# Hybrid decoder block on one core: two weight-gain sums moved within the first projection, the rotary tables moved behind the first value head

## The chip, the core and the metric

The kernel runs on one core of a Trainium2 chip. The metric is the device time of one execution in microseconds; before the change it is 2252.84 us, the median of three runs (2250.17 to 2253.78). The engines of the core work through queues of their own: PE (TensorE: matrix products and transposes), DVE (VectorE: elementwise work), ACT (ScalarE: copies, casts and functions), POOL (GpSimd: elementwise work, and a queue that issues loads) and SP (SyncE: a queue that issues loads). Each takes its instructions in the order in which they were written into its queue.

## The reference, cut to what matters

One decoder block on 512 tokens of width 2048. The condition `c` gives six vectors of 2048 (shift, scale and gate, for each half of the block); the normalised input, scaled and shifted by them, goes through one projection into attention heads (`aq`, `ak`, `av`) and heads of a gated recurrence (`gq`, `gf`, `gi`, `gg`). Queries and keys of the attention get a rotary embedding on their first 32 channels.

```python
mod = silu(c) @ w_ada + b_ada
shift1, scale1, gate1, shift2, scale2, gate2 = split(mod, 6)
h = rms_norm(x, norm1_w) * (1 + scale1) + shift1
aq, ak, av, gq, gf, gi, gg = split(h @ w_in, ...)
ang = pos[..., None] * inv_freq            # 16 frequencies
aq = rope_partial(rms_norm(aq), cos(ang), sin(ang)); ak likewise
attn = dilated_attention(aq, ak, av)
ho = hgrn2(gq, gf, gi, lb)                 # gated recurrence
x = x + gate1 * (concat(attn, norm(ho) * silu(gg)) @ w_out)
x = x + gate2 * (square(relu((rms_norm(x, norm2_w) * (1 + scale2) + shift2) @ w_ff1)) @ w_ff2)
```

## The kernel before

Every float32 product is done as three products of rounded parts: a weight tile is split into `whi` (a cast on ACT) and `wlo` (the rest, on DVE), the input tile into `hi` and `lo`, and PE adds hi·whi, lo·whi and hi·wlo. The input dimension of 2048 is worked through in 16 tiles `k` of 128.

**The first projection** (`first_steps`, lines 730 to 908) makes the first four forget-gate heads (four banks `bt`, 512 columns) and two query heads (two banks `bc`, 256 columns). Its order on PE, SP, ACT and DVE is that of the code, as it stands under a manual schedule; POOL's is set by the planner. The weights are scaled by `g1c`, one value per input channel, which is norm1 times (1 + scale1). Because `g1c` comes itself out of a product with `w_ada`, it is made in eight blocks `b` of 256 channels while the projection runs: block `b` gives `g1c` for the tiles k = 2b and 2b + 1, and `split_w(k)` (line 757) can start only when it is there. Blocks 0, 1, 3, 5 and 7 are summed on PE: `summed` (line 792) multiplies, and `summed_out` (line 801) copies the sums out on ACT (line 803), transposes them on PE (line 806), reduces them on DVE (line 807) and calls `finish_scale` (two small DVE instructions, lines 813 and 814). Blocks 2, 4 and 6 are summed on DVE: `gathered` (line 816) does 16 scaled additions, and `gathered_out` (line 826) has four PE transposes and four ACT sums (`to_cols`, lines 144 and 147), then `finish_scale`. `fetch_block` (line 740) issues a block's eight loads on SP, `fetch_pair` (line 752) the projection's weights on POOL.

`dense(k)` (line 865) is the projection's product for one tile, in three runs of six matmuls: hi·whi, lo·whi, hi·wlo. What is handed in as `between` is issued before the third run. `split_x` splits the input tiles (cast on ACT, rest on DVE), `turn_x` transposes an input tile on PE and copies it out. The loop over pairs at line 880 puts these together; b = k0 / 2 + 1 is the block that the next pair needs.

`shift_steps(n)` (line 876) takes n steps of a background list: the sums for `shift1` on DVE, one step being one load of 128x512 on SP (line 117) and one scaled addition (lines 122 and 124), with transposes and ACT sums after each 16 (lines 144, 147). There are four such blocks of 512 channels. The **second projection** (`first_groups`, line 247) follows with the same input tiles and takes eight steps per pair; as a block of shifts is done, `shifted` (line 278) rewrites the input tiles with the shift in. Its PE work ends with the transposes of the last block. The **first value projection** (line 1006, `project(5120)`, "value head") uses the shifted tiles; its evacuation is at line 346. Behind the first projections, the planner orders DVE, ACT and POOL by the code's order as priority, with its own estimate of times, and gives out the buffers; PE's order from line 1004 on is that of the code.

**The rotary tables** (lines 962 to 995) stand between the two first projections: the angles, reduced in range, on DVE (28 instructions on 128x64 and smaller, most of them on the tile `rp`), two sines on ACT (lines 985, 986), `sinT` and `cosT` on DVE, and eight products with the norm weights on POOL into `rot_w` (line 995). Three of the eight buffers of the pool `wk` (512 columns each) hold `cosT`, `sinT` and `rp`. `rot_w` is first read by `qk_norm` (line 362), for the first query heads behind line 1011. The recurrent heads (`hgrn_head`, line 520) take their tiles `kk`, `Sx`, `z` and `mt` from the same pool.

Of the kernel before, what the change touches and what calls it, by code (L numbers as in the profile page):

```python
# [8 lines left out]
F32 = mybir.dt.float32  # L9
F32R = mybir.dt.float32r  # L10
I32 = mybir.dt.int32
AF = mybir.ActivationFunctionType
ALU = mybir.AluOpType
AX = mybir.AxisListType

P = 128
D = 2048
S = 512
NK = D // P
NT = S // P  # L20
# [5 lines left out]
MAGIC = 12582912.0  # L26
PI2 = 6.283185307179586
PI2_1 = 6.28125
PI2_2 = 0.0019350051879882812
PI2_3 = 3.019916050073166e-07  # L30
# [18 lines left out]
def hybrid_block(ctx, tc, x, c, positions, norm1_w, w_ada, b_ada, w_in, q_norm_w, k_norm_w,  # L49
# [3 lines left out]
    pe, dve, act, pool = nc.tensor, nc.vector, nc.scalar, nc.gpsimd  # L53
# [14 lines left out]
    ca = pa.enter_context(tc.tile_pool(name="ca", bufs=1))  # L68
# [31 lines left out]
    n2c, aoc, hgc, posc = cols[:, 0:16], cols[:, 16:24], cols[:, 40:41], cols[:, 44:48]  # L100
    rw = ca.tile([P, 2, 32], F32, name="rw")
# [3 lines left out]
    ifq = ca.tile([P, 16], F32, name="ifq")  # L105
# [125 lines left out]
    def work(name, dt=F32):  # L231
        return wk.tile([P, 512], dt, name=name, tag="wk")
# [403 lines left out]
    def hgrn(fs, qs, vs, rs, lead=0):  # L636
        ss = sm.tile([P, 4, NT], F32, name="hss", bufs=2)
        for h in range(4):
            yield from hgrn_head(h, fs[h], qs[h], vs, ss, 0 if h else lead)
        rstd_of(rs.rearrange("p t h -> p (t h)"), ss.rearrange("p t h -> p (t h)"), 16, 1.0 / DH)  # L640
# [89 lines left out]
    def first_steps(c_f, c_q):  # L730
# [7 lines left out]
        on_pe = (0, 1, 3, 5, 7)  # L738
# [18 lines left out]
        def split_w(k):  # L757
            parts[k] = [_split(nc, wr, raw[:, k % 2], raw.shape[2], None, g1c[:, k:k + 1]) for raw in wraws[k - k % 2]]

        def split_x(ks):  # L760
            for k in ks:
                hl = pair(k)
                hhi.append(hl[0])
                hlo.append(hl[1])
                split_to(hl, xnT[k])
# [18 lines left out]
        def turn_x(q, j, tag="bg"):  # L784
            pt = bank("ptx", tag=tag)
            for ti in range(NT):
                pe.transpose(pt[:, ti * P:(ti + 1) * P], xs[ti][q][:, j * P:(j + 1) * P], ident)
            t = slot("xnT")
            (dve.tensor_copy if q == 1 else act.copy)(t, pt)
            xnT.append(t)  # L790
# [25 lines left out]
        def gathered(b, ks):  # L816
            if b not in accs:
                accs[b] = [work("acc")[:, 0:256] for _ in range(2)]
            for k in ks:
                raw, acc = raws[b][k // 2][:, k % 2], accs[b][k % 2]  # L820
                if k < 2:
                    dve.tensor_scalar(acc, raw, sc[:, k:k + 1], None, op0=ALU.mult)
                else:
                    dve.scalar_tensor_tensor(acc, raw, sc[:, k:k + 1], acc, op0=ALU.mult, op1=ALU.add)
# [40 lines left out]
        def dense(k, between=None):  # L865
            fine, coarse = parts.pop(k)
            first, last = k == 0, k == NK - 1
            for n, (hs, w) in enumerate(((hhi, 0), (hlo, 0), (hhi, 1))):
                for banks, ws in ((bt, fine), (bc, coarse)):
                    for j in range(len(banks)):  # L870
                        pe.matmul(banks[j], lhsT=ws[w][:, j * P:(j + 1) * P], rhs=hs[k], start=first and n == 0,  # L871
                                  stop=last and n == 2)
                if n == 1 and between:
                    between()

        def shift_steps(n):
            for _ in range(n):
                bg_step()

        for k0 in range(0, NK, 2):  # L880
            b = k0 // 2 + 1
            if k0 + 4 < NK:
                fetch_pair(k0 + 4)
            if b < 8 and b not in on_pe:
                gathered(b, range(8, NK))
            if 0 < k0 < NK - 2:
                split_x((k0 + 2, k0 + 3))
            if k0 in (0, 4):
                scale_x(2 + k0 // 4, range(NT))
            dense(k0, lambda: turn_x(2 + k0 // 6, (k0 - 2) % 4) if 2 <= k0 <= 8 else None)  # L890
            if k0 in (0, 4, 10):
                summed((1, 3, 7)[k0 // 4], range(4))
            if 2 <= k0 <= 8:
                turn_x(2 + k0 // 6, (k0 - 2) % 4 + 1)
            shift_steps(5 if k0 == 10 else 0)
            dense(k0 + 1, lambda: None if b > 7 else (summed_out if b in on_pe else gathered_out)(b))
            if k0 == 6:
                summed(5, range(4))
            if b + 2 < 8:
                fetch_block(b + 2)  # L900
            if k0 + 2 < NK:
                split_w(k0 + 2)
                if b + 1 < 8 and b + 1 not in on_pe:
                    gathered(b + 1, range(8))
                shift_steps(4 if k0 >= 10 else 0)
                split_w(k0 + 3)
        shift_steps(4)
# [29 lines left out]
    with tc.issue_after(mod_cols.last.ins):  # L937
        posf = ca.tile([NT, P], F32, name="posf")
        dve.tensor_copy(posf, posi)
        ps_v = bank("ps_v")  # L940
        pe.transpose(ps_v[:, 0:P], rows, ident)
        pe.transpose(ps_v[:, P:P + NT], posf, ident[0:NT, 0:NT])
        dve.tensor_copy(cols[:, 0:41], ps_v[:, 0:41])
        dve.tensor_copy(posc, ps_v[:, P:P + NT])


        lbm = ca.tile([P, 8], F32, name="lbm")
        lbe = ca.tile([P, 16], F32, name="lbe")
        lb = ca.tile([P, 8], F32, name="lb")
        omlb = ca.tile([P, 8], F32, name="omlb")  # L950
        l0, l1 = cols[:, 24:32], cols[:, 32:40]
        dve.tensor_tensor(lbm, l0, l1, op=ALU.max)
        dve.tensor_tensor(lbe[:, 0:8], l0, lbm, op=ALU.subtract)
        dve.tensor_tensor(lbe[:, 8:16], l1, lbm, op=ALU.subtract)
        act.activation(lbe, lbe, AF.Exp)
        dve.tensor_tensor(lbm, lbe[:, 0:8], lbe[:, 8:16], op=ALU.add)
        dve.reciprocal(lbm, lbm)
        dve.tensor_tensor(lb, lbe[:, 0:8], lbm, op=ALU.mult)
        dve.tensor_scalar(omlb, lb, -1.0, 1.0, op0=ALU.mult, op1=ALU.add)


        rot_w = ca.tile([P, 2, 4, NT, 16], F32, name="rot_w")
        cosT, sinT = (work(n)[:, 0:NT * 16].rearrange("p (t f) -> p t f", f=16) for n in ("cosT", "sinT"))
        rp = work("rp")
        ang, rem, half, co = (rp[:, i * 64:(i + 1) * 64] for i in range(4))
        for ti in range(NT):
            dve.tensor_scalar(ang[:, ti * 16:(ti + 1) * 16], ifq, posc[:, ti:ti + 1], None, op0=ALU.mult)
        dve.tensor_copy(rem, ang)
        turns = []
        for e in (20, 10, 0):  # L970
            u = float(2.0 ** e)
            k = rp[:, (4 + len(turns)) * 64:(5 + len(turns)) * 64]
            dve.tensor_scalar(k, rem, 1.0 / (PI2 * u), MAGIC, op0=ALU.mult, op1=ALU.add)
            dve.tensor_scalar(k, k, -MAGIC, None, op0=ALU.add)
            if e:
                dve.scalar_tensor_tensor(rem, k, -PI2 * u, rem, op0=ALU.mult, op1=ALU.add)
            turns.append((k, u))
        for part in (PI2_1, PI2_2, PI2_3):
            for k, u in turns:
                dve.scalar_tensor_tensor(ang, k, -part * u, ang, op0=ALU.mult, op1=ALU.add)  # L980

        dve.tensor_scalar(half, ang, 0.5, None, op0=ALU.mult)
        dve.scalar_tensor_tensor(co, half, -1.0, half, op0=ALU.mult, op1=ALU.max)
        dve.tensor_scalar(co, co, -1.0, PI2 / 4, op0=ALU.mult, op1=ALU.add)
        act.activation(half, half, AF.Sin)
        act.activation(co, co, AF.Sin)
        sT = sinT.rearrange("p t f -> p (t f)")
        cT = cosT.rearrange("p t f -> p (t f)")
        dve.scalar_tensor_tensor(sT, half, 2.0, co, op0=ALU.mult, op1=ALU.mult)
        dve.tensor_tensor(co, half, half, op=ALU.mult)  # L990
        dve.tensor_scalar(cT, co, -2.0, 1.0, op0=ALU.mult, op1=ALU.add)
        for i in range(2):
            for j, (tab, h) in enumerate(((cosT, 0), (sinT, 1), (cosT, 1), (sinT, 0))):
                w = rw[:, i:i + 1, h * 16:(h + 1) * 16].broadcast_to([P, NT, 16])
                pool.tensor_tensor(rot_w[:, i, j], tab, w, op=ALU.mult)

    bt, bc = first_groups(4096 + 512, 3072 + 256, lambda k0: None, shift_block)
    f1 = keep(bt, "f")
    hq0 += keep(bc, "gq", QS)
# [7 lines left out]
    while bgw:  # L1007
        bg_step()
    bgw[:] = later
    tasks.append(hgrn(f0, hq0, hv0, hrs[0], 3))  # L1010
    q0 = qk(0, "aq", 0)
    k0_ = qk(1024, "ak", 1)
# [581 lines left out]
```

## Time and profile before

| | before |
|---|---|
| median of three runs | 2252.84 us (2250.17 to 2253.78) |
| the profiled execution | 2256.4 us, of which its span 2254.6 us |
| PE busy | 2218.2 us, 98% of the span |
| DVE busy | 1785.1 us, 79% |
| ACT busy | 1090.7 us, 48% |
| POOL busy | 460.5 us, 20% |
| mean granted clock of PE | 0.998 of full speed |

The profile is of one execution. A busy time is the sum of an engine's instructions. Matmuls follow each other in a pipeline, and one's duration reaches into the next one's, so that busy PE is not PE at its peak: a run of four 128x512 matmuls starts 0.91 us before the next run, though each row shows 0.39 us. The granted clock is given as a share of 2.4 GHz.

### The profile page before, as it was taken

The page shows a single profiled execution, that of the slowest core. Times are in us where ns is not written, and L with a number is a line of the kernel's source. Part 1 is how long each engine was busy: PE and PEld are TensorE (multiplying, and loading weights), DVE is VectorE, ACT ScalarE, POOL GpSimd, SP SyncE. Part 2 cuts the span into 40 slices and gives each one's busy share as a digit, 9 for nine tenths or more (in the row PEclk, how much of TensorE's full clock was granted, in tenths as well). Part 3 has the DMA queues.
Part 4 walks back from the last instruction along what each step waited for, and adds up shares of the span by engine and source line. Part 5 has one row for each costly group of instructions (what it writes and reads, how often), then busy time and mean ns, then how long its engine had stood idle before and what let it go on. Part 6 is the DMA issues. An engine that isn't in the chain of part 4 may idle for free.

```text
span 2254.6 us, 33232 instructions
## 1 busy us (share of the span) xinstructions
PE 2218.2 (98%) x11919; PEld 1825.3 (81%) x11919; DVE 1785.1 (79%) x2700; ACT 1090.7 (48%) x1912; POOL 460.5 (20%) x693
## 2 busy tenths in 40 slices
PE   6999999999999999999999999999999999999999
PEld 4787888888888888878887888888887888888887
DVE  5699988678977566778657988998897779967878
ACT  5456444534444554457444565565654333443332
POOL 1220031001210000013232322332332222222221
PEclk9999999999999999999999999999999999999999
DMA  9787655556564258738879789889979987998884
GB/s 336 259 312 278 210 174 188 165 172 207 173 205 146 75 187 285 242 110 311 323 273 345 282 299 385 316 300 354 343 289 354 374 309 264 342 346 315 304 295 167
DMA packets 258101, 598.31 MB, mean 265 GB/s; under 512 B 23220, under 2 KB 40384, under 8 KB 257936
## 3 DMA queue, kind: packets, MB, share of 16 engines
q1 hardware_dynamic: 179008, 321.46, 41.9%
q0 software_dynamic: 73856, 265.23, 32.1%
q10 hardware_dynamic: 5072, 9.51, 1.3%
q8 instruction: 94, 1.54, 0.3%
q14 instruction: 71, 0.58, 0.1%
HBM read 518.49 MB, written 77.61 MB: 264 GB/s over the span
## 4 chain that ended last, share of the span: by engine, by line
PE 86%; DMA 5%; DVE 5%; issue 3%; ACT 1%; POOL 1%; SPq 0%; ACTq 0%; DVEq 0%; POOLq 0%
PE f L1352 14%; PE f L1350 14%; PE f L1351 14%; PE prj L198 8%; PE prj L200 8%; PE prj L199 8%; PE f L208 2%; PE f L206 2%; PE f L207 2%; PE prj L871 2%; PE prj L206 1%; PE prj L207 1%; DMA Fl<-f_lod 1%; PE prj L208 1%; DMA wraw<-in_w_ff_dram 1%
## 5 line engine op out<-in xcount | busy, mean ns | idle before, releaser
L1334 ACT CAST vhi<-raw 128x1024 fp32r<-128x1024 f32 x392 | 413.3, 1055 | 521.5 <-PE f L1352 416.4
L1335 DVE TENSOR_TENSOR vlo<-raw,vhi 128x1024 fp32r<-128x1024 f32 x392 | 476.6, 1225 | 141.7 <-ACT vhi L1334 141.3
L1352 PE MATMUL f<-vhi,Fl 128*128 128x512 f32 x1376 | 535.5, 389 | 1.2 <-DMA Fl<-f_lod 1.2
L1351 PE MATMUL f<-vlo,Fh 128*128 128x512 f32 x1376 | 535.8, 389 | 0.5 <-DVE vlo L1335 0.4
L1350 PE MATMUL f<-vhi,Fh 128*128 128x512 f32 x1376 | 535.9, 389 | 0.1
L40 ACT CAST whi<-wraw 128x512 fp32r<-128x512 f32 x304 | 187.1, 621 | 368.9 <-PE prj L200 279.2
L198 PE MATMUL prj<-whi,hi 128*128 128x512 f32 x896 | 359.8, 402 | 0.8 <-ACT aq L346 0.5
L200 PE MATMUL prj<-whi,lo 128*128 128x512 f32 x896 | 350.0, 391 | 0.2 <-DVE lo L240 0.2
L199 PE MATMUL prj<-wlo,hi 128*128 128x512 f32 x896 | 349.1, 390 | 0.0
L41 DVE TENSOR_TENSOR wlo<-wraw,whi 128x512 fp32r<-128x512 f32 x304 | 210.3, 696 | 154.1 <-ACT whi L40 149.2
L1351 PEld LDWEIGHTS f<-vlo,Fh 128*128 128x128 f32 x1376 | 258.4, 188 | 55.4 <-DVE vlo L1335 2.1
L1352 PEld LDWEIGHTS f<-vhi,Fl 128*128 128x128 f32 x1376 | 258.3, 188 | 55.1 <-DMA Fl<-f_lod 1.7
L1350 PEld LDWEIGHTS f<-vhi,Fh 128*128 128x128 f32 x1376 | 258.3, 188 | 53.8 <-ACT a L1530 0.5
L1318 DVE TENSOR_TENSOR raw<-raw,raw 128x1024 f32<-128x1024 f32 x224 | 271.2, 1224 | 6.7 <-DMA raw<-in_w_ff_dram 6.3
L124 DVE SCALAR_TENSOR_TENSOR acc<-araw,sc,acc 128x512 f32<-128x512 f32 x280 | 201.7, 751 | 23.2 <-DMA araw<-in_w_ada_dram 22.7
L200 PEld LDWEIGHTS prj<-whi,lo 128*128 128x128 f32 x896 | 168.2, 188 | 36.8 <-DVE lo L240 0.6
L198 PEld LDWEIGHTS prj<-whi,hi 128*128 128x128 f32 x896 | 168.4, 188 | 35.9 <-ACT ak L346 0.9
L199 PEld LDWEIGHTS prj<-wlo,hi 128*128 128x128 f32 x896 | 168.5, 188 | 32.6
L1296 POOL DMA_DIRECT2D Fh<-f_hid x112 | 79.0, 705 | 432.2 <-PE f L1352 418.6
L208 PE MATMUL f<-hi,wlo 128*128 128x512 f32 x256 | 99.9, 390 | 2.3 <-DVE wlo L41 2.3
L206 PE MATMUL f<-hi,whi 128*128 128x512 f32 x256 | 100.3, 392 | 0.0
L207 PE MATMUL f<-lo,whi 128*128 128x512 f32 x256 | 99.6, 389 | 0.0
(339 smaller groups left out, 2996.4 us busy)
## 6 DMA issues: line engine op xcount, KB each, us to landing
raw<-in_w_ff_dram SPq DMA_DIRECT2D x224, 512.0 KB, 11.0
araw<-in_w_ada_dram SPq DMA_DIRECT2D x384, 256.0 KB, 4.5
Fh<-f_hid POOLq DMA_DIRECT2D x112, 512.0 KB, 6.8
Fl<-f_lod POOLq DMA_DIRECT2D x112, 512.0 KB, 8.0
wraw<-in_w_in_dram SPq DMA_DIRECT2D x90, 512.0 KB, 4.6
Fh<-h_hid POOLq DMA_DIRECT2D x60, 512.0 KB, 6.8
Fl<-h_lod POOLq DMA_DIRECT2D x60, 512.0 KB, 7.6
f_hid<-part POOLq DMA_DIRECT2D x48, 512.0 KB, 7.4
```

The lines of the kernel that those rows point to most:

```text
L40: nc.scalar.copy(hi, src)
L41: _split.low = (eng or nc.vector).tensor_tensor(lo, src, hi.bitcast(F32), op=ALU.subtract)
L124: dve.scalar_tensor_tensor(acc, raw[:, k - k0], vec[:, k:k + 1], acc, op0=ALU.mult, op1=ALU.add)
L198: pe.matmul(banks[ti], lhsT=hi[:, ts], rhs=whi, start=first, stop=False)
L199: pe.matmul(banks[ti], lhsT=hi[:, ts], rhs=wlo, start=False, stop=False)
L200: pe.matmul(banks[ti], lhsT=lo[:, ts], rhs=whi, start=False, stop=last)
L1318: dve.tensor_tensor(dst, a, b, op=ALU.subtract)
L1334: cast_done.append(act.copy(hi, src))
L1335: split_done.append(dve.tensor_tensor(lo, src, hi.bitcast(F32), op=ALU.subtract))
L1350: pe.matmul(banks[t], lhsT=fh[u][a][:, ts], rhs=whi[:, a], start=first, stop=False)
L1351: pe.matmul(banks[t], lhsT=fh[u][a][:, ts], rhs=wlo[:, a], start=False, stop=False)
L1352: pe.matmul(banks[t], lhsT=fl[u][a][:, ts], rhs=whi[:, a], start=False, stop=end)
```

## The change

Four things move; nothing is computed otherwise. In the first projection block 6 is gathered half a pair sooner: its first half before `dense(8)`, the second between `split_w(10)` and `split_w(11)`. Blocks 5 and 7 are finished one tile sooner, inside `dense(8)` and `dense(12)` and not inside `dense(9)` and `dense(13)`. The five shift steps before `dense(11)` become two before it and three behind it, ahead of `split_w(12)`. The 34 lines of the rotary tables go, unchanged, from between the two first projections to behind the first value projection and what remains of the background list.

```diff
-            if b < 8 and b not in on_pe:
+            if b in (2, 4):
                 gathered(b, range(8, NK))
             if 0 < k0 < NK - 2:
                 split_x((k0 + 2, k0 + 3))
+            if k0 == 8:
+                gathered(6, range(8))
             if k0 in (0, 4):
                 scale_x(2 + k0 // 4, range(NT))
-            dense(k0, lambda: turn_x(2 + k0 // 6, (k0 - 2) % 4) if 2 <= k0 <= 8 else None)
+
+            def inside():
+                if 2 <= k0 <= 8:
+                    turn_x(2 + k0 // 6, (k0 - 2) % 4)
+                if k0 in (8, 12):
+                    summed_out((5, 7)[k0 // 12])
+
+            dense(k0, inside)
             if k0 in (0, 4, 10):
                 summed((1, 3, 7)[k0 // 4], range(4))
             if 2 <= k0 <= 8:
                 turn_x(2 + k0 // 6, (k0 - 2) % 4 + 1)
-            shift_steps(5 if k0 == 10 else 0)
-            dense(k0 + 1, lambda: None if b > 7 else (summed_out if b in on_pe else gathered_out)(b))
+            shift_steps(2 if k0 == 10 else 0)
+            dense(k0 + 1, lambda: gathered_out(b) if b in (2, 4, 6) else summed_out(b) if b in (1, 3) else None)
...
             if k0 + 2 < NK:
+                shift_steps(3 if k0 == 10 else 0)
                 split_w(k0 + 2)
-                if b + 1 < 8 and b + 1 not in on_pe:
+                if k0 in (0, 4):
                     gathered(b + 1, range(8))
+                elif k0 == 8:
+                    gathered(6, range(8, NK))
                 shift_steps(4 if k0 >= 10 else 0)
                 split_w(k0 + 3)
...
-        rot_w = ca.tile([P, 2, 4, NT, 16], F32, name="rot_w")
-        cosT, sinT = (work(n)[:, 0:NT * 16].rearrange("p (t f) -> p t f", f=16) for n in ("cosT", "sinT"))
-        rp = work("rp")
...
     bt, bc = first_groups(4096 + 512, 3072 + 256, lambda k0: None, shift_block)
...
     bgw[:] = later
+    rot_w = ca.tile([P, 2, 4, NT, 16], F32, name="rot_w")
+    cosT, sinT = (work(n)[:, 0:NT * 16].rearrange("p (t f) -> p t f", f=16) for n in ("cosT", "sinT"))
+    rp = work("rp")
...
     tasks.append(hgrn(f0, hq0, hv0, hrs[0], 3))
```

## Rows read from the trace of the kernel before

**Rows 1.** PE's waits: who waited for whom, total, times, longest (us).
```profile
PE prj L871 <- ACT whi L43: 3.5, 2, 2.3
...
PE f L208 <- DVE wlo L41: 2.3, 2, 1.2
```
**Rows 2.** Busy time by stretch: length, busy us (instructions) by engine, clock, DMA, GB/s.
```profile
97.00:101.50 4.50, 4.43 (x12) 3.49 (x13) 4.45 (x8) 2.72 (x7) 0.00 (x0) 0.62 0.44 161
101.50:175.00 73.50, 73.50 (x332) 60.57 (x331) 65.14 (x143) 42.15 (x87) 15.58 (x24) 1.00 0.84 291
175.00:186.00 11.00, 9.62 (x43) 7.28 (x42) 11.00 (x20) 8.72 (x14) 0.53 (x1) 1.00 0.88 306
186.00:400.00 214.00, 213.47 (x1791) 175.70 (x1791) 185.34 (x399) 99.82 (x292) 29.42 (x53) 1.00 0.63 205
```
**Rows 3.** Timeline, 88 to 98 us: start, duration, instruction, [idle before <- releaser].
```profile
88.75 3.26 DVE L824 SCALAR_TENSOR_TENSOR acc<-araw,sc,acc 128x256 f32<-128x256 f32 x8
...
92.78 0.60 PE L144 MATMUL pc<-ident,acc 128*128 128x128 f32 x4
...
93.91 2.08 DVE L124 SCALAR_TENSOR_TENSOR acc<-araw,sc,acc 128x512 f32<-128x512 f32 x3
...
94.26 0.19 ACT L147 ACTIVATION_READ_ACCUMULATOR pc<-pc 128x1 f32 x1
95.89 0.17 DVE L813 TENSOR_TENSOR g1c<-g1c,bcol 128x2 f32<-128x2 f32 x1
...
96.29 2.13 ACT L43 ACTIVATE whi<-wraw,g1c 128x512 fp32r<-128x512 f32 x4 [1.84 <-DVE g1c L814]
...
97.07 1.39 PE L871 MATMUL prj<-hi,whi 128*128 128x512 f32 x4 [2.30 <-ACT whi L43]
```
**Rows 4.** Timeline, 76 to 88 us, same columns.
```profile
76.89 0.60 PE L787 MATMUL ptx<-ident,xs 128*128 128x128 f32 x4
...
77.24 1.18 PE L871 MATMUL prj<-hi,wlo 128*128 128x512 f32 x4
...
77.52 0.59 ACT L789 COPY xnT<-ptx 128x512 f32<-128x512 f32 x1 [2.01 <-PE ptx L787]
...
79.07 1.17 PE L871 MATMUL prj<-hi,whi 128*128 128x512 f32 x4
...
79.84 0.38 ACT L803 COPY acc<-gp 128x256 f32<-128x256 f32 x1
...
82.33 0.17 DVE L807 TENSOR_REDUCE g1c<-pc 128x2 f32<-128x8 f32 x1 [5.81 <-PE pc L806]
...
83.74 1.19 PE L871 MATMUL prj<-hi,whi 128*128 128x512 f32 x4
...
88.06 1.93 PE L798 MATMUL gp<-araw,scz 128*32 128x256 f32 x32
```
**Rows 5.** Timeline of PE, 182 to 186 us.
```profile
183.91 0.66 PE L144 MATMUL pc<-ident,acc 128*128 128x128 f32 x4 [1.15 <-DVE acc L138]
...
185.72 0.50 PE L198 MATMUL prj<-whi,hi 128*128 128x512 f32 x1 [0.22 <-ACT f L704]
```
**Rows 6.** Busy time of the instructions on `rp` alone: length, DVE, ACT, clock, DMA, GB/s.
```profile
104.00:132.00 28.00, 5.71 (x28) 0.50 (x2) 1.00 0.59 195
```
**Rows 7.** Timeline, 108 to 129 us.
```profile
108.62 0.37 DVE L967 TENSOR_SCALAR rp<-ifq,cols 128x16 f32<-128x16 f32 x2
...
125.53 1.28 ACT L985 ACT_TABLE_LOAD   x1
...
127.55 0.23 DVE L989 SCALAR_TENSOR_TENSOR sinT<-rp 128x64 f32<-128x64 f32 x1 [2.13 <-ACT rp L986]
...
128.44 1.06 DVE L122 TENSOR_SCALAR acc<-araw,sc 128x512 f32<-128x512 f32 x2
```
**Rows 8.** Busy time of line 995 alone: length, POOL, clock, DMA, GB/s.
```profile
104.00:132.00 28.00, 4.00 (x8) 1.00 0.59 195
```
**Rows 9.** Timeline, 227 to 252 us.
```profile
227.84 0.59 ACT L346 COPY gi<-prj 128x512 f32<-128x512 f32 x1 [0.78 <-PE prj L200]
...
251.55 0.28 DVE L558 TENSOR_TENSOR mt<-pA,hgm 128x128 f32<-128x128 f32 x1
```

More of the change, by code (lines that the diff above doesn't have):

```diff
@@ L959, in hybrid_block @@
         dve.tensor_scalar(omlb, lb, -1.0, 1.0, op0=ALU.mult, op1=ALU.add)
-        rot_w = ca.tile([P, 2, 4, NT, 16], F32, name="rot_w")
-        cosT, sinT = (work(n)[:, 0:NT * 16].rearrange("p (t f) -> p t f", f=16) for n in ("cosT", "sinT"))
-        rp = work("rp")
[L965 to L995, printed above, removed]
     bt, bc = first_groups(4096 + 512, 3072 + 256, lambda k0: None, shift_block)
@@ L1009, in hybrid_block @@
     bgw[:] = later
+    rot_w = ca.tile([P, 2, 4, NT, 16], F32, name="rot_w")
+    cosT, sinT = (work(n)[:, 0:NT * 16].rearrange("p (t f) -> p t f", f=16) for n in ("cosT", "sinT"))
+    rp = work("rp")
+    ang, rem, half, co = (rp[:, i * 64:(i + 1) * 64] for i in range(4))
+    for ti in range(NT):
+        dve.tensor_scalar(ang[:, ti * 16:(ti + 1) * 16], ifq, posc[:, ti:ti + 1], None, op0=ALU.mult)
+    dve.tensor_copy(rem, ang)
+    turns = []
+    for e in (20, 10, 0):
+        u = float(2.0 ** e)
+        k = rp[:, (4 + len(turns)) * 64:(5 + len(turns)) * 64]
+        dve.tensor_scalar(k, rem, 1.0 / (PI2 * u), MAGIC, op0=ALU.mult, op1=ALU.add)
+        dve.tensor_scalar(k, k, -MAGIC, None, op0=ALU.add)
+        if e:
+            dve.scalar_tensor_tensor(rem, k, -PI2 * u, rem, op0=ALU.mult, op1=ALU.add)
+        turns.append((k, u))
+    for part in (PI2_1, PI2_2, PI2_3):
+        for k, u in turns:
+            dve.scalar_tensor_tensor(ang, k, -part * u, ang, op0=ALU.mult, op1=ALU.add)
+    dve.tensor_scalar(half, ang, 0.5, None, op0=ALU.mult)
+    dve.scalar_tensor_tensor(co, half, -1.0, half, op0=ALU.mult, op1=ALU.max)
+    dve.tensor_scalar(co, co, -1.0, PI2 / 4, op0=ALU.mult, op1=ALU.add)
+    act.activation(half, half, AF.Sin)
+    act.activation(co, co, AF.Sin)
+    sT = sinT.rearrange("p t f -> p (t f)")
+    cT = cosT.rearrange("p t f -> p (t f)")
+    dve.scalar_tensor_tensor(sT, half, 2.0, co, op0=ALU.mult, op1=ALU.mult)
+    dve.tensor_tensor(co, half, half, op=ALU.mult)
+    dve.tensor_scalar(cT, co, -2.0, 1.0, op0=ALU.mult, op1=ALU.add)
+    for i in range(2):
+        for j, (tab, h) in enumerate(((cosT, 0), (sinT, 1), (cosT, 1), (sinT, 0))):
+            w = rw[:, i:i + 1, h * 16:(h + 1) * 16].broadcast_to([P, NT, 16])
+            pool.tensor_tensor(rot_w[:, i, j], tab, w, op=ALU.mult)
     tasks.append(hgrn(f0, hq0, hv0, hrs[0], 3))
```

## The prediction

> **What bounds the kernel now.** I read the list of TensorE's waits first, then the busy time by stretches, then the timeline around each wait. TensorE (PE) is busy for 98% of the span, so a change can gain only where PE stands still or is clocked down. Of the waits behind the start-up, the longest in the stretch that the diff touches is that of the first projection on ACT's `whi` (line 43), 2.3 us [rows 1]. In the table of stretches PE has no idle time at all from 101.5 to 175 us, about 1.4 us between 175 and 186, and half a microsecond in the 214 us after that [rows 2]. So the change can act at four places only: in the first projection (74 to 108 us), in the second (to 183), at the border at 183 to 186, and in the first value projection, where the rotary tables go.
>
> The 2.3 us wait is read backwards in the timeline [rows 3]. `dense(12)` starts at 97.07, 0.78 us after ACT began `whi` at 96.29; this waited for `finish_scale(6)` on DVE, whose first instruction ran at 95.89. Its input had been ready since 94.26 + 0.19 = 94.45, when ACT's last read of the four sums ended. The 1.44 us between are DVE's own queue: the second half of block 6 (88.75), two splits, and then five shift sums, the last three at 93.91 for 2.08 us. Right behind the wait the granted clock is 0.62 of full speed over 4.5 us [rows 2], that is, some of it at the lower of the two levels (1.2 GHz instead of 2.4).
>
> **Block 5 inside dense(8).** `summed_out(5)` moves from the third run of `dense(9)` to that of `dense(8)`, behind `turn_x`. ACT takes both copies in written order: first the copy of `turn_x`'s output, at 77.52 for 0.59 us, then the copy of block 5's sums, which takes 0.38 us (at 79.84 before). So the sums are in SBUF at 77.52 + 0.59 + 0.38 = 78.49. PE's next instruction is now their transposition; before, it went on with the third run at 77.24 [rows 4]. It stands still for about 1 us, and with 0.17 us for two transposes (half of the 0.35 between `turn_x`'s four at 76.89 and the next run) it resumes at 78.66: +1.42. What comes back: `dense(9)` took 79.07 to 83.74 = 4.67 us with the transposes and a short wait for `whi` at its end; a product without them took 83.74 to 88.06 = 4.32 [rows 4]. That is -0.35. Net **+1.0**, rounded down. Lower bound +0.7, if ACT overlaps the ends of its two copies; upper +1.4, if nothing comes back.
>
> **Block 6 earlier.** Its eight additions cost 3.26 us [rows 3]; the first half goes to where DVE idled for 5.81 us before 82.33 [rows 4], so it is free there, and the second half takes its place behind `split_w(10)`. PE reaches block 6's transposes at 92.78 + 1.0 = 93.78. DVE has then long finished block 6 and, with two shift sums instead of five in front, waits for ACT. From transposes to the start of the next product it is 1.67 us to the last read (92.78 to 94.45), 0.40 to `whi` (95.89 to 96.29) and 0.78 to PE, together 2.85 [rows 3]: 93.78 + 2.85 = 96.63 instead of 97.07, **-0.44** in all, the +1.0 included. PE's gap shrinks from 2.30 to 96.63 - (94.77 + 1.0) = 0.86 us. The three shift sums put behind (2.08 us) now stand before `wlo` of `dense(12)` on DVE, which PE wants only in its third run, some 2.7 us after its start: covered, with about a microsecond to spare.
>
> **The clock.** A gap of 1.15 us at 183.91 with transposes behind it left the clock at 1.00 [rows 2, 5]; the one of 2.30 did not. With 0.86 I expect no fall. The fall cost 4.50 x (1 - 0.62) = 1.71 us: **-1.71** (0 if it falls all the same). The Trainium skill (TensorE: Matmul & The Clock Gate, Part 4: PE-mode transpose) says that transposes do not engage full speed, as they do not count as busy in the same way. By that rule the new wait inside `dense(8)`, framed by six transposes, would be a longer rest than it looks; it is the first rival. The row at 183.91 speaks against it, for there a longer gap had four transposes behind it.
>
> **Block 7 earlier.** The two transposes only change from `dense(13)` to `dense(12)`; `whi` of `dense(14)` may come early enough to save its wait. I take **0** (-0.25 to +0.25). First stage together: -0.44 - 1.71 = **-2.15**.
>
> **Rotary tables.** Their instructions on the `rp` tile are 5.71 us of DVE and 0.50 of ACT [rows 6], with a table load of 1.28 on ACT, spread from 108.62 on, with a wait of 2.13 us in DVE's queue for ACT's sine before 127.55 [rows 7]. Only behind them, at 128.44, does DVE begin the second block of shift sums. PE never waited there, but the chain of shift sums ends in the transposes at 183.91, for which PE waited 1.15 us, and then 0.22 us more for ACT's evacuation at 185.72 [rows 2, 5]. With DVE about 8 us less loaded (5.71 + 2.13) and PE only 2.15 earlier, the last block of sums should be there in time. I take **-1.15**; bounds 0 (ACT's evacuations late in their turn) and -1.37. In the new place DVE and ACT do the same work beside the first value projection and the first recurrent head, ACT with perhaps a second table load to go back; it is busy there for 99.8 us of 214. Until 400 us PE loses 0.5 us there in all [rows 2], so I take 0 for it. If the cover were gone, one wait for the sine would cost up to 2.13. POOL's eight products, 4.00 us [rows 8], move past its weight loads of the second projection, which PE's unbroken stretch shows to be early anyway: 0.
>
> **Sum:** -2.15 - 1.15 = **-3.3 us**: 2254.6 - 3.3 = 2251.3 of span. The profiled execution took 2256.4, 3.6 above the median of the timed runs (2252.84); against that median it is 2249.5. A difference within 0.2% (4.5 us) can't be told from no change in a measurement of this kernel. The forecast lies inside it; its own range is 2248.4 to 2252.
>
> **Rivals.** *The clock falls at the new wait.* Then 1.71 us come back: -1.6, or 2251.2. For it: a wait with transposes on both sides, by the rule above. Against: the row at 183.91. Chance 0.06.
>
> *The shift sums stay the bound.* The second projection starts 2.15 us earlier, but the sums are fed by loads whose share of the DMA engines is already 0.84 over 101.5 to 175 [rows 2]; if they end when they did, PE waits 1.15 + 2.15 us at the border and nothing is left: 2252.8. Chance 0.12.
>
> *More than the border.* Terms at their good ends: -2.15 - 0.3 (block 5) - 0.25 - 1.37 = -4.1, and a DVE that is ahead also meets one of the two later waits on `wlo` (1.2 us at most each [rows 1]): -5.3, or 2247.5. For it: nothing else holds PE. Against: those waits lie hundreds of microseconds later, behind other work. Chance 0.31.
>
> *Slower: the tables hold work buffers.* `cosT`, `sinT` and `rp` take three of the eight work buffers until POOL's last product. The first recurrent head needs five (`kk`, `Sx`, three `z`) and then more: the masked product at 251.55, by then 248.2. If the chain only starts with the value head's evacuation (227.84 - 3.3 = 224.5) and takes as long as before (108.62 to 128.5, 19.9 us, plus 4.0 on POOL), it ends at 248.4, just at that point [rows 7 to 9]. From there each microsecond is one of PE's. With half as much again on a DVE that is busier there, the overrun is 10 us, with a fall of the clock 11.9: +8.6, or 2261.4. Against: the inputs are there from 108 us on, and DVE has holes before. Chance 0.09.
>
> **How the numbers follow.** Forecast 0.42 (2249.5), clock rival 0.06, shift sums 0.12, more 0.31, slower 0.09. Faster by over 0.2%: 0.31. Within: 0.42 + 0.06 + 0.12 = 0.60. Slower: 0.09. The range runs from 2245.0, under the third rival's time with a microsecond of spread per term, to 2255.0, over the second with a fall of the clock; it leaves out the slow rival and the far end of the third.
>
> **What would show it.** Right: a PE gap of about 1 us inside `dense(8)` before the transposes of line 806; a gap of 0.7 to 1.2 us at the start of `dense(12)` with the clock at 1.00 behind it; `dense(14)` some 2 us earlier; the wait before 183.91 gone or below half a microsecond; no new wait from 186 to 290. Wrong: a lower clock after either gap, the border's wait grown by what the first stage gained, or a wait at the first head's products.

## The result and the profile after

The changed kernel takes 2250.19 us, the median of 14 executions (2248.48 to 2253.10), beside 2252.65 us (2249.49 to 2255.72) of the kernel before, run in turn with it. The ratio is 0.9986, with a 95% interval from 0.998 to 0.9993: about 3.2 us faster (1.6 to 4.5); the two medians are 2.5 us apart. The gain lies inside the bound of 0.2%, and the time is 0.7 us from the 2249.5 that was forecast. The profiled execution took 2249.24 us, of which 2247.5 us are span.

Two profiled executions differ by more than the change, here by 7.1 us. So the places below are counted from the start of `dense(8)`, where the first edited step acts. That start is at 74.03 us before and 73.43 us after:

| start of, counted from `dense(8)` | before | after | difference |
|---|---|---|---|
| `dense(10)` | 9.72 | 10.69 | +0.97 |
| `dense(12)` | 23.04 | 22.46 | -0.58 |
| `dense(14)` | 33.57 | 31.44 | -2.13 |
| first product of the queries | 155.65 | 151.40 | -4.25 |
| the product behind the wait for the queries' evacuation | 208.75 | 205.56 | -3.19 |

The last row is the gain of the change: 3.19 us, against 3.3 forecast. Of the other 3.9 us, 0.6 lie ahead of `dense(8)`, where nothing was edited, and 3.3 behind the queries' wait. There the two profiles differ in the waits between 978 and 1706 us, and those differ without any edit: the one for `wlo` at about 1009 us was 0.91 us long in the changed kernel and 2.40 in the one without the sine (below), whose DVE, ACT and POOL have the same instructions in the same order behind the value head.

The rows from which the table comes, in the timeline of PE before (start, duration, instruction, [idle before <- releaser]):

```profile
74.03 1.20 PE L871 MATMUL prj<-hi,whi 128*128 128x512 f32 x4
...
107.60 1.19 PE L871 MATMUL prj<-hi,whi 128*128 128x512 f32 x4
...
229.68 0.39 PE L198 MATMUL prj<-whi,hi 128*128 128x512 f32 x1
...
282.78 0.50 PE L198 MATMUL prj<-whi,hi 128*128 128x512 f32 x1 [0.49 <-ACT aq L346]
```

and after:

```profile
73.43 1.21 PE L871 MATMUL prj<-hi,whi 128*128 128x512 f32 x4
...
104.87 1.19 PE L871 MATMUL prj<-hi,whi 128*128 128x512 f32 x4
...
224.83 0.39 PE L198 MATMUL prj<-whi,hi 128*128 128x512 f32 x1
...
278.99 0.50 PE L198 MATMUL prj<-whi,hi 128*128 128x512 f32 x1 [0.49 <-ACT aq L346]
```

PE's waits of the kernel after between 75 and 330 us (who waited for whom, total, times, longest) answer [rows 1]:

```profile
PE pc L806 <- ACT acc L803: 0.9, 1, 0.9
PE prj L871 <- ACT whi L43: 0.9, 1, 0.9
...
PE prj L198 <- ACT gi L346: 0.3, 1, 0.3
```

The 2.30 us are now 0.9. The first row is new, inside `dense(8)`, and so is the last one, at the value head's evacuation; the prediction had named "no new wait from 186 to 290" as a sign of being right. The border's two waits are gone. The table of stretches of the kernel after (columns as in [rows 2]):

```profile
95.50:100.00 4.50, 4.11 (x19) 3.36 (x20) 4.50 (x8) 3.06 (x7) 0.00 (x0) 1.00 0.50 181
...
175.00:186.00 11.00, 11.00 (x52) 9.11 (x51) 10.02 (x18) 8.73 (x22) 0.00 (x0) 1.00 0.96 338
186.00:400.00 214.00, 213.00 (x1797) 175.11 (x1796) 185.01 (x418) 98.14 (x284) 33.78 (x62) 1.00 0.62 203
```

The clock is 1.00 behind the wait where it was 0.62, PE is busy without a hole from 175 to 186, and from 186 to 400 it has lost 1.00 us where it lost 0.53. The steps themselves, in the timeline of the kernel after:

```profile
76.33 0.60 PE L787 MATMUL ptx<-ident,xs 128*128 128x128 f32 x4
...
77.45 0.38 ACT L803 COPY acc<-gp 128x256 f32<-128x256 f32 x1
...
77.88 0.44 PE L806 MATMUL pc<-ident,acc 128*128 128x128 f32 x2 [0.95 <-ACT acc L803]
78.08 1.17 PE L871 MATMUL prj<-hi,wlo 128*128 128x512 f32 x4
...
94.73 0.16 DVE L813 TENSOR_TENSOR g1c<-g1c,bcol 128x2 f32<-128x2 f32 x1 [5.34 <-ACT pc L147]
95.00 2.08 DVE L124 SCALAR_TENSOR_TENSOR acc<-araw,sc,acc 128x512 f32<-128x512 f32 x3
...
95.89 1.20 PE L871 MATMUL prj<-hi,whi 128*128 128x512 f32 x4 [0.89 <-ACT whi L43]
...
177.93 0.69 DVE L138 TENSOR_TENSOR acc<-acc 128x512 f32<-128x512 f32 x1
...
179.42 0.61 PE L208 MATMUL prc<-hi,wlo 128*128 128x512 f32 x2
179.87 0.39 PE L198 MATMUL prj<-whi,hi 128*128 128x512 f32 x1
...
181.24 0.60 PE L144 MATMUL pc<-ident,acc 128*128 128x128 f32 x4
```

These rows answer [rows 3 to 5]. DVE now waits for ACT (5.34 us) before `finish_scale(6)`, and the three shift sums stand behind it. The last sum of the second projection is done at 177.93 + 0.69 = 178.62; PE comes to its transposes at 181.24, with no wait. In PE's queue six products of the value head, from 179.87, now stand ahead of the transposes. They are not what removed the wait: without them PE would have come at 179.87, still 1.25 us behind the sum.

The tables, in the same timeline, answer [rows 7 to 9]:

```profile
193.19 0.65 DVE L991 TENSOR_SCALAR rp<-ifq,cols 128x16 f32<-128x16 f32 x4
...
217.04 1.28 ACT L1009 ACT_TABLE_LOAD   x1
218.33 0.26 ACT L1009 ACTIVATE rp<-rp 128x64 f32<-128x64 f32 x1
...
220.50 1.28 ACT L717 ACT_TABLE_LOAD   x1
...
223.60 0.56 ACT L346 COPY gi<-prj 128x512 f32<-128x512 f32 x1
224.77 0.72 ACT L717 ACTIVATE sg<-gq,scol 128x512 f32<-128x512 f32 x1 [0.60 <-DVE gq L718]
225.40 0.57 ACT L346 COPY gi<-prj 128x512 f32<-128x512 f32 x1
...
225.29 0.39 PE L200 MATMUL prj<-whi,lo 128*128 128x512 f32 x1
226.02 0.50 PE L198 MATMUL prj<-whi,hi 128*128 128x512 f32 x1 [0.34 <-ACT gi L346]
226.35 0.39 PE L199 MATMUL prj<-wlo,hi 128*128 128x512 f32 x1
```

The tables' work begins at 193.19, in holes of DVE ahead of its place in the code, and ends on POOL at 222.54 (the last four products begin at 221.02 and take 1.52 us). ACT loads a table for the sine and another to go back. It is then late with the value head's evacuation, for which PE waits. Before, ACT waited there 0.78 us for PE [rows 9].

### The profile page after: what moved, and what is told of

It reads as the page before. It is cut to its first block, busy times and chain, and to the rows that moved or that the text cites. A ratio compares the mean times of both kernels' runs of the same rounds, so it can differ in the third digit from the quotient of the medians.

```text
span 2247.5 us, 33209 instructions
## 1 busy us (share of the span) xinstructions
PE 2215.8 (99%) x11919; PEld 1824.7 (81%) x11919; DVE 1785.9 (79%) x2700; ACT 1093.1 (49%) x1913; POOL 460.5 (20%) x693
## 4 chain that ended last, share of the span: by engine, by line
PE 73%; issue 5%; DMA 5%; DVE 4%; POOL 1%; ACT 1%; SPq 0%; POOLq 0%; DVEq 0%; ACTq 0%
PE f L1362 12%; PE f L1360 12%; PE f L1361 12%; PE prj L198 8%; PE prj L200 8%; PE prj L199 7%; PE f L208 2%; PE f L207 2%; PE f L206 2%; DMA f_lod<-fs 1%; DMA Fl<-f_lod 1%; DMA wraw<-in_w_ff_dram 1%; PE pho L628 1%; PE po L441 1%; DVE vlo L1345 1%
```

## The experiments

The expectations count from the start of `turn_x(3, 2)`, which is 2.9 us behind that of `dense(8)` (3.1 us in the last four kernels of the table, where the sums' transposes come ahead of it). The table counts all from `dense(8)`. "Border" is the time from `dense(14)` to the first product of the queries, so it holds the second projection, the border and the products of the value head; with no stop of PE in it, it is 119.96 to 120.02 us. "Value head" is the time from there to the product behind the queries' wait; it holds the stops for the value head's evacuation, and without them it is 53.10 to 53.14 us.

| kernel | `dense(14)` | border | value head | in all | ratio to before (95%) |
|---|---|---|---|---|---|
| before | 33.57 | 122.08 | 53.10 | 208.75 | |
| after | 31.44 | 119.96 | 54.16 | 205.56 | 0.9986 (0.998 to 0.9993) |
| tables in the old place | 31.33 | 124.32 | 53.10 | 208.75 | 0.9995 (0.9986 to 1.0005) |
| only the tables moved | 33.58 | 119.96 | 54.17 | 207.71 | 0.9996 (0.9986 to 1.0005) |
| only the shift sums split | 30.51 | 122.86 | 53.12 | 206.49 | 0.999 (0.9981 to 1.0) |
| only block 6 moved | 30.51 | 123.90 | 53.12 | 207.54 | 0.9986 (0.9977 to 0.9996) |
| block 5 in the old place | 30.59 | 119.96 | 54.21 | 204.76 | 0.998 (0.9971 to 0.9989) |
| block 7 in the old place | 31.33 | 119.99 | 54.18 | 205.51 | 0.9979 (0.9968 to 0.9989) |
| without the sine | 31.44 | 119.96 | 53.14 | 204.54 | 0.9984 (0.9975 to 0.9993) |
| sums ahead of `turn_x` | 30.15 | 119.99 | 54.21 | 204.35 | 0.9976 (0.9966 to 0.9986) |
| and block 6 finished sooner | 28.90 | 119.99 | 54.17 | 203.06 | 0.9967 (0.9956 to 0.9977) |
| and tables before the value head | 28.93 | 120.02 | 53.10 | 202.06 | 0.9965 (0.9953 to 0.9978) |
| or tables behind its evacuation | 28.89 | 119.99 | 56.15 | 205.03 | 0.998 (0.9971 to 0.9989) |

The times are too coarse to order neighbours (0.1% is 2.25 us); the orders below come from the traces.

**The tables back in their old place.** The changed kernel, with the 34 lines between the two first projections again.

```diff
+        rot_w = ca.tile([P, 2, 4, NT, 16], F32, name="rot_w")
...
     bt, bc = first_groups(4096 + 512, 3072 + 256, lambda k0: None, shift_block)
...
     bgw[:] = later
-    rot_w = ca.tile([P, 2, 4, NT, 16], F32, name="rot_w")
...
```

> The changed kernel with the rotary tables back between the two first projections. Places are told from the start of turn_x inside dense(8) (76.89 us before, 76.33 in the changed kernel); dense(14) begins 30.71 us behind it before and 28.54 in the changed kernel, the evacuation of the first queries releases PE 205.89 and 202.66 behind it. Theory (the tables load DVE and so delay the shift sums): dense(14) stays at 28.5, the wait before the last shift transposes is back with about 1.1 us, the queries come at about 203.6, 2.2 us before the kernel before. Rival (the lead of the first projection alone frees the border): no wait there, queries at about 202.3.

Both theories expected a net gain, and there was none: 208.75 in both kernels. `dense(14)` starts 2.24 us sooner, and the border takes 2.24 us more. The timeline of PE in this kernel, and its busy time from 180 to 186 us (columns as in [rows 2]):

```profile
179.43 0.73 PE L208 MATMUL prc<-hi,wlo 128*128 128x512 f32 x2 [0.52 <-DVE wlo L44]
181.96 1.11 PE L144 MATMUL pc<-ident,acc 128*128 128x128 f32 x4 [1.80 <-DVE acc L138]
...
180.00:186.00 6.00, 4.20 (x15) 3.34 (x15) 6.00 (x10) 6.00 (x12) 0.53 (x1) 0.72 0.96 327
```

PE waits twice for DVE, which has no idle time in these 6 us, and then runs at a mean clock of 0.72, in part at 1.2 GHz. What the first projection gained is paid at the border, as the prediction's second rival, the shift sums as the bound, had it. That it comes out even is luck: the same wait of 1.80 us in the kernel with only the sums split (below) is not followed by a fall of the clock, and the border gives back 0.78 us there. A fall costs 1.55 to 1.68 us (last section). By an estimate from these numbers, DVE took back 0.6 to 0.7 of the 2.24 us, and the clock the rest. The sums did not end when they did before, either: counted from `dense(8)`, the last one is done at 109.2 here, 109.8 before and 105.2 in the changed kernel.

**Only the tables moved.** The kernel before, with the 34 lines in the new place and nothing else.

> The kernel before with only the rotary tables moved. Theory: first projection as before (gap of 2.3 us at dense(12), clock fallen behind it, dense(14) at 30.7), no wait at the last shift transposes (1.15 before) nor behind them (0.22), but the wait of 0.34 us at the value head's evacuation as in the changed kernel: queries at about 204.9, 1.0 us sooner than before. Rival (DVE's load by the tables had nothing to do with it, the loads of the shift weights set the sums): the wait of about 1.1 us stays and the time is 0.3 us longer than before.

The border takes 119.96 us as in the changed kernel, 2.12 less than before, and the value head 1.07 more. The net gain of 1.04 is what the theory expected, but its parts are not: 2.12 at the border where 1.37 (1.15 and 0.22) was expected, and 1.07 lost at the value head where 0.34 was. The first projection keeps its wait of 2.3 us.

**Only the shift sums split.**

```diff
-            shift_steps(5 if k0 == 10 else 0)
+            shift_steps(2 if k0 == 10 else 0)
...
             if k0 + 2 < NK:
+                shift_steps(3 if k0 == 10 else 0)
                 split_w(k0 + 2)
```

> The kernel before with only the five shift steps split into two and three. Theory (the last three sums in DVE's queue are what finish_scale(6) waited for): the gap at dense(12) falls from 2.3 to 0.9 us, the clock stays at 1.00, dense(12) comes 1.4 us sooner and dense(14) 3.1 sooner (at 27.6), sooner than in the changed kernel, which pays 0.9 us for block 5 inside dense(8). Border wait as before. About 3.1 us faster. Rival (block 6 has to be gathered sooner too): gap of 1.5 us or more with the clock fallen, under 1 us gained.

`dense(14)` starts 3.06 us sooner, as expected, and 0.93 sooner than in the changed kernel. The border, expected as before, gives 0.78 us back. Its timeline, PE and DVE:

```profile
176.91 0.48 DVE L44 SCALAR_TENSOR_TENSOR wlo<-wraw,g1c,whi 128x256 fp32r<-128x256 f32 x1
177.30 0.68 DVE L41 TENSOR_TENSOR wlo<-wraw,whi 128x512 fp32r<-128x512 f32 x1
177.44 0.73 PE L208 MATMUL prc<-hi,wlo 128*128 128x512 f32 x2
177.91 1.41 DVE L124 SCALAR_TENSOR_TENSOR acc<-araw,s1c,acc 128x512 f32<-128x512 f32 x2
179.23 0.68 DVE L138 TENSOR_TENSOR acc<-acc 128x512 f32<-128x512 f32 x1
179.97 0.66 PE L144 MATMUL pc<-ident,acc 128*128 128x128 f32 x4 [1.80 <-DVE acc L138]
```

This is the lock. PE's last two products need a `wlo` that DVE finishes at 177.39; behind it in DVE's queue stand a split, two sums and the last addition, until 179.91. PE has 0.73 us of work for these 2.52. So a PE that comes sooner meets DVE at the `wlo`, and the wait of 1.80 cannot grow: what is lost beyond it shows as a wait for `wlo`, as with the tables in the old place.

**Only block 6 moved.**

```diff
-            if b < 8 and b not in on_pe:
+            if b in (2, 4):
                 gathered(b, range(8, NK))
...
+            if k0 == 8:
+                gathered(6, range(8))
...
+                elif k0 == 8:
+                    gathered(6, range(8, NK))
```

> The kernel before with only block 6 gathered half a pair sooner; five shift steps stay in front of finish_scale(6). Theory (DVE's queue as a whole decides, so either cure will do): the five sums end at about 93.1, before ACT's 94.45, so that the gap is 0.9 us and the clock stays, dense(14) 3.1 us sooner than before (27.6). Rival (the sums in front are the cause whatever lies before them, as they wait for their loads): gap of 1.5 us or more, clock fallen, under 1 us gained.

Again -3.06 us at `dense(14)`: either cure is enough, and the two together bring no more. The border takes 1.82 us more than before. The wait is 1.80 as in the kernel with the split sums, but here the clock falls behind it:

```profile
180.00:186.00 6.00, 5.29 (x18) 4.08 (x19) 6.00 (x11) 5.33 (x13) 0.52 (x1) 0.72 0.99 341
```

In the kernel with the split sums the same stretch has a clock of 1.00.

**Block 5 back in `dense(9)`**, in the changed kernel.

```diff
-                if k0 in (8, 12):
-                    summed_out((5, 7)[k0 // 12])
+                if k0 == 12:
+                    summed_out(7)
...
-            dense(k0 + 1, lambda: gathered_out(b) if b in (2, 4, 6) else summed_out(b) if b in (1, 3) else None)
+            dense(k0 + 1, lambda: gathered_out(b) if b in (2, 4, 6) else summed_out(b) if b in (1, 3, 5) else None)
```

> The changed kernel with one thing undone: block 5's summed_out runs in dense(9) again, not in dense(8). All times are counted from the start of the eight transposes of turn_x(3, 2). Theory A: block 5's move cost PE 0.95 us of waiting and brought nothing, since the shift split alone and block 6's move alone each cured the first projection's gap. Then dense(14) starts at about 27.6 (28.54 in the changed kernel), the queries' evacuation wait stands near 201.7 (202.66), and the kernel is about 1 us faster than the changed one, some 4 us faster than the one before. Theory B: block 5's place is what lets block 6's second half and wlo of dense(10) come early; undone, a wait for DVE at dense(12) grows from 0.89 towards 2.30 and dense(14) starts at 28.5 or later, no gain.

Theory A: `dense(14)` starts 0.85 us sooner, the whole 0.80. Block 5's move costs its wait and brings nothing.

**Block 7 back in `dense(13)`.** The same edit for `k0 == 12`.

> The changed kernel with one thing undone: block 7's summed_out runs in dense(13) again, not in dense(12). The prediction put this part at 0 (-0.25 to +0.25). If so, dense(14) starts between 28.3 and 28.8 after the start of turn_x(3, 2) (28.54 in the changed kernel) and the time is the same. Rival: block 7 late makes whi of dense(14) late, a wait like that of dense(12) (about 0.9 us) appears at dense(14), and it is 29.2 to 29.5.

0.11 us, within the bounds of the prediction; no wait at `dense(14)`.

**The sums ahead of `turn_x`**, in the changed kernel.

```diff
             def inside():
-                if 2 <= k0 <= 8:
-                    turn_x(2 + k0 // 6, (k0 - 2) % 4)
                 if k0 in (8, 12):
                     summed_out((5, 7)[k0 // 12])
+                if 2 <= k0 <= 8:
+                    turn_x(2 + k0 // 6, (k0 - 2) % 4)
```

> The changed kernel with two calls exchanged inside dense(8): block 5's transposes ahead of those of turn_x. Theory A: the 0.95 us wait is PE waiting for ACT, which copies turn_x's output (0.59 us) before the sums (0.38 us). Exchanged, ACT copies the sums first, about 1 us before PE comes to them, the wait is gone, dense(14) starts at 27.4 to 27.6 instead of 28.54 and the queries' evacuation wait stands near 201.6 instead of 202.66: about 1 us faster than the changed kernel. Theory B: ACT's copy waits for something else (a buffer, DVE's sums), and the wait of PE stays at 0.9 or more wherever the transposes stand; nothing gained.

Timeline of ACT and PE in this kernel:

```profile
75.53 0.36 ACT L803 COPY acc<-gp 128x256 f32<-128x256 f32 x1
...
76.99 0.38 PE L806 MATMUL pc<-ident,acc 128*128 128x128 f32 x2
```

ACT has the sums ready at 75.89, 1.1 us before PE wants them: the wait came from the order of the two copies alone. The gain is 1.29 us at `dense(14)`: the wait, and some 0.4 us that block 5's old place costs (against 30.59).

**Block 6 finished sooner as well.** The exchange, and `gathered_out(6)` ahead of `dense(11)`, not in its third run.

```diff
+            if k0 == 10:
+                gathered_out(6)
-            dense(k0 + 1, lambda: gathered_out(b) if b in (2, 4, 6) else summed_out(b) if b in (1, 3) else None)
+            dense(k0 + 1, lambda: gathered_out(b) if b in (2, 4) else summed_out(b) if b in (1, 3) else None)
```

> As with the exchange in dense(8), and block 6's transposes moved from the third run of dense(11) to ahead of dense(11), half a product (about 3 us) sooner. Theory A: the 0.89 us wait at dense(12) is the chain from block 6's transposes by ACT and finish_scale to whi; begun earlier it ends before PE comes, that wait goes too, dense(14) starts at about 26.5 to 26.7 (28.54 in the changed kernel) and the queries' evacuation wait near 200.6 to 200.8 (202.66): 2 us faster than the changed kernel. Rival: another wait takes its place, ACT's evacuation of the transposes or DVE's split for dense(11), or the border's wait for the shift sums comes back, since PE comes there 2 us sooner: then dense(14) may gain but the queries stay at 201.6 or later.

Theory A, and some 0.7 us more than it expected. PE has no hole from 76 to 100 us in this kernel, and the border keeps its 119.99 though PE comes there 2.5 us sooner:

```profile
76.00:100.00 24.00, 24.00 (x139) 19.12 (x138) 19.11 (x46) 9.50 (x21) 9.15 (x17) 1.00 0.98 333
```

**Without the sine.** The changed kernel with copies in the sines' place; the sine is left out, and with it ACT's two loads.

```diff
-    act.activation(half, half, AF.Sin)
-    act.activation(co, co, AF.Sin)
+    act.activation(half, half, AF.Copy)
+    act.activation(co, co, AF.Copy)
```

> The changed kernel with the two sine activations replaced by plain copies of the same size, so the sine itself is left out and the tables hold other numbers; everything else stands in the same order, only ACT's two loads of 1.28 us, for the sine and back for the sigmoid, are gone. Theory A: PE's wait of 0.34 us for the value head's evacuation (150 us after the start of turn_x(3, 2)) is the price of these two loads on ACT, which stands before the evacuation in the queue. Then the wait is gone, the queries' evacuation wait stands at 202.3 instead of 202.66, and the time falls by some 0.3 us, less than a comparison of times can show. Rival: the wait comes from DVE's later gate (gq) or from the order of the four evacuations among the sigmoids; then it stays at 0.3 or more.

The wait is gone, so the loads are its cause, but 1.02 us are gained and not 0.34. In part they act through DVE: ahead of the second evacuation ACT waits 0.60 us for DVE's gate `gq` in the changed kernel (224.77 above), and 0.16 here. PE's timeline without the sine, at the place of the rows of 225.29 to 226.35 above:

```profile
225.17 0.39 PE L200 MATMUL prj<-whi,lo 128*128 128x512 f32 x1
225.40 0.39 PE L198 MATMUL prj<-whi,hi 128*128 128x512 f32 x1
225.62 0.39 PE L199 MATMUL prj<-wlo,hi 128*128 128x512 f32 x1
```

From start to start it is 0.23 and 0.22 us here, and 226.02 - 225.29 = 0.73 and 0.33 in the changed kernel: one stop with 0.34 us of listed idle time costs 0.61. A second stop, at 227.11, costs the other 0.41.

**The tables before the value head**, on the kernel with block 6 finished sooner: the 34 lines stand between the second projection and `project(5120)`.

```diff
     later.insert(0, shift_through(4096 + 512))
+    rot_w = ca.tile([P, 2, 4, NT, 16], F32, name="rot_w")
...
     hv0 = evac(project(5120, tok_mm, 2.0), "gi")
...
-    rot_w = ca.tile([P, 2, 4, NT, 16], F32, name="rot_w")
```

> The kernel with block 6's transposes sooner, and the rotary tables written between the second projection and the first value head instead of behind it, so that the sines run before the sigmoids of the decay and ACT needs one load less. Theory A: the 0.34 us wait goes, and DVE, with nothing of the tables before 150 us, still ends the shift sums in time: queries' evacuation wait at 199.6 to 199.7 instead of 199.98, no wait at the border, the fastest kernel of all, 6 to 7 us under the kernel before. Rival: with part of the 5.71 us of the tables in front of the last block of shift sums, DVE is again the bound at the border: a wait of 1 to 2 us for the sums, queries at 201 to 202, 1 to 2 us slower than the kernel with block 6's transposes sooner.

Theory A, with 1.0 us gained and not 0.3. Timeline of ACT:

```profile
191.71 1.28 ACT L1003 ACT_TABLE_LOAD   x1
...
200.89 1.28 ACT L495 ACT_TABLE_LOAD   x1
```

The second load is one that the changed kernel has as well, for the sigmoids of the decay, so one load in all is saved, and neither stands near the evacuation. The border is 120.02. Its median, 2244.78 us (2243.08 to 2247.25) beside 2254.28, is the lowest of all, though the timed ratio does not part it from the kernel with block 6 finished sooner; by the traces it gains 6.69 us on the kernel before and 3.50 on the changed one.

**The tables behind the evacuation**, on the kernel with block 6 finished sooner: the lines in the changed place, but inside a block that holds back what they give to ACT until behind the value head's last evacuation. So only the two sines, and what needs them, come later; DVE's work on the angles still runs from 191.5 to 215 us, and the expectation, which has all of the tables' work held back, is tested for the sines only.

```diff
+    with tc.issue_after(evacuated[0].ins):
-    rot_w = ca.tile([P, 2, 4, NT, 16], F32, name="rot_w")
+        rot_w = ca.tile([P, 2, 4, NT, 16], F32, name="rot_w")
...
```

> The kernel with block 6's transposes sooner, and the tables' work held back until the first evacuation of the value head, so that the sines run some 10 us later and the first recurrent head's chain (kk, Sx, z), which needs the tables' work buffers, begins about 11 us later on DVE. Theory A, the price that the prediction's slow rival named: the head's first masked product comes late and each microsecond past its due point is one of PE's; waits of several microseconds between 225 and 260 us, queries' evacuation wait at 203 to 210 instead of 199.98, slower by 3 to 10 us. Rival: PE's queries take as long as the head needs, the products are fed later but in time; no wait, and with the 0.34 us gone as well the queries stand at 199.6.

Between the two: waits do appear, and cost 3.05 us on the 53.10 that the stretch takes without a wait. Timeline:

```profile
225.66 1.28 ACT L1012 ACT_TABLE_LOAD   x1
...
235.48 0.67 POOL L547 MEMSET Sx<- 128x512 f32 x1
...
244.04 0.46 PE L517 MATMUL pA<-z 128*32 128x32 f32 x32 [0.70 <-DVE z L544]
...
246.11 0.88 DVE L558 TENSOR_TENSOR mt<-pA,hgm 128x128 f32<-128x128 f32 x4
...
262.72 0.68 PE L605 MATMUL pD<-z 128*128 128x128 f32 x4 [2.07 <-DVE z L544]
```

`Sx` is cleared at 235.48 (222.49 in the changed kernel), and PE waits for the head's `z`, not for the masked products, which begin at 246.11, no later than elsewhere (248.01 in the changed kernel). What makes `z` late, the tables' buffers, POOL's queue, in which the clearing of `Sx` stands behind the tables' products, or ACT's second load, now at 255.02, was not separated.

## Why the prediction was right, and where it was not

The total was right, 3.3 us forecast and 3.19 measured, but two of its terms missed by a microsecond each, with opposite signs. That they cancel, 0.97 us more at the border and 1.06 less at the tables' new place, is luck.

**Block 5.** Resumption of PE was put at +1.42 behind `turn_x`; it is 78.08 - 76.33 = 1.75 against 0.35 before, +1.40. Net +1.0 was forecast, +0.97 is measured at `dense(10)`, and undone it gives 0.85 back. Right. That block 5's place was of no use to the rest was not seen.

**Block 6 and the shift sums.** -0.44 forecast at `dense(12)`, -0.58 measured, with a wait of 0.89 (0.86 forecast). The working gave the credit to both parts together. Each alone does it, as the two runs with -3.06 show, and this was not in the prediction.

**The clock.** No fall, as forecast, behind waits of 0.95 and 0.89 us. Between `dense(12)` and `dense(14)` 33.57 - 23.04 = 10.53 us became 8.98, -1.55 (with no fall, -1.71 was forecast). Both traces with the wait of 2.30 us show the fall behind it, but a wait of 2.40 us in the kernel without the sine has none; so whether every execution of the kernel before pays it, and the change gains it each time, is not shown. The first rival rested on a rule of the Trainium skill (TensorE: Matmul & The Clock Gate, Part 4: PE-mode transpose). The trace doesn't bear it out here: a wait of 0.95 us framed by six transposes left the clock at 1.00. It is no test of the rule by itself, as no wait of up to 1.35 us in these traces, with transposes or without, was followed by a fall. First stage together: -2.15 forecast, -2.13 measured.

**Block 7** at 0: 0.11 when undone. Right.

**The border.** Here the step failed that added up listed waits: -1.15, with the bounds 0 and -1.37. It is -2.12, outside the bounds. The mechanism was right, DVE relieved of the tables, as the kernels with the tables moved show, the one with only them moved above all, with 119.96. Whether it is their 5.71 us of work or the 2.13 us for which DVE waited for the sine, no run separates. The size was off, because the idle time of a row isn't what a stop costs. In the kernel before, PE goes from 182.14, its last run of the projection, to 184.54, the first product of the value head, in 2.40 us, with the row at 183.91 [rows 5] between:

```profile
182.14 0.61 PE L208 MATMUL prc<-hi,wlo 128*128 128x512 f32 x2
...
184.54 0.50 PE L198 MATMUL prj<-whi,hi 128*128 128x512 f32 x1
```

Without a wait the run takes 179.87 - 179.42 = 0.45 and the four transposes 181.59 - 181.24 = 0.35 by the starts in the trace of after: 1.60 us are lost, where the row lists 1.15. At 185.72 it is 0.50, by the same reckoning, where the row lists 0.22. Together 2.10.

**The tables in their new place.** The step "ACT with perhaps a second table load to go back; it is busy there for 99.8 us of 214 ... so I take 0" failed; it is +1.06. A mean over 214 us says nothing of the 8 us before an evacuation, in which ACT has two loads, two sines, the first two of four sigmoids and the sums for them to do. The loads are rows of 1.28 us, and the sine follows 218.33 - 217.04 = 1.29 behind the start of its load. The Trainium skill (ScalarE: Activation LUTs, What ACT_TABLE_LOAD costs) adds a drain of about 1.38 us to the load; no such time shows here.

**The rivals.** *The shift sums stay the bound* (0.12) is in part what happens when the tables stay: the gain of the first stage was lost there, but some 1.6 of the 2.24 us to a fall of the clock. So its condition was the table move, and the prediction had priced it as if it could strike with the tables moved. It also laid the bound to the loads; what has no idle time there is DVE. *More than the border* (0.31) did not occur at 2247.5, though its cause, DVE ahead, did. The later waits on `wlo` from which it hoped for 1.2 us differ from trace to trace without any edit. *The tables hold work buffers* (0.09) rested on the chain starting at the evacuation; in the trace it starts 30 us sooner, at 193.19. With its sines held back it does cost waits, 3.05 us, not at the point named, the masked products, but at `z`; the chain as a whole so late was not run.

What is not settled: whether the gains of the traces carry to the end of the program in full. The timed ratios allow it in each case, but their intervals are 3 to 6 us wide.

## What to carry to other kernels

Price a stop of PE by the distance of starts before and behind it, not by its listed idle time: the end of a matmul's row reaches some 0.16 us into the next, and the first one behind a stop takes longer. Of two waits in a row, the second can take back what is gained at the first: make room on the engine that PE meets next (here DVE's queue of shift sums) before counting a gain in front of it. A function that needs a table of its own on ACT did best here ahead of a load that was due anyway, and away from evacuations.

## What was not expected of the hardware

The same wait is followed by a fall of the clock in one kernel's trace and not in another's. In the 13 traces of this study PE has 21 waits of 1.80 to 2.40 us behind the first 60 us. Behind 11 of them the granted clock falls to 0.50 (1.2 GHz), behind 10 it stays at 1.00; the wait of 2.00 us for `s` near 1215 us, the same in all kernels, has both. None of the waits of 0.9 to 1.35 us is followed by a fall. A fall costs 1.55 us by the starts of the first projection (1.62 against the kernel with only the sums split, where block 7 has not moved either), and 6.00 x (1 - 0.72) = 1.68 by the clock of the border's six microseconds, so that much of an execution can come or go with no change that explains it.
